# Summing a norm's squares on GpSimd, at later steps, with the inverse norm kept in PSUM

## The chip, the cores and the metric

The program runs on eight cores of one Trainium2 chip, one copy per core, each with its own 2112 tokens; the cores share no data. The metric is the device time of the slowest core in microseconds. Most executions agree within 0.3%, but some fall in a second, slower state, in which one die or both show a lower granted TensorE clock.

Engines are named as in the profile: PE is TensorE, DVE is VectorE, ACT is ScalarE, POOL is GpSimd; SP issues DMAs, PEld is PE's weight load, and a q at the end marks an engine's sequencer. A line in order of time gives start and length in us, engine, line of kernel.py, operation, output<-inputs, shape and count; in brackets stands how long the engine had been idle before and what ended that.

## The reference, cut to what matters

```python
def rmsnorm(x, g):
    xf = x.astype(jnp.float32)
    r = lax.rsqrt(jnp.mean(xf * xf, axis=-1, keepdims=True) + EPS)
    return (xf * r).astype(x.dtype) * g

for l in range(DEPTH):                                   # DEPTH = 4
    h = rmsnorm(x, p['norm1'][l])
    z = h @ p['w_in'][l]
    ...                                                  # pooling, spatial gate, conv: a_out, b_out, c_out
    x = x + jnp.concatenate([a_out, b_out, c_out], axis=-1) @ p['w_out'][l]
    h2 = rmsnorm(x, p['norm2'][l])
    up = h2 @ p['w_up'][l]
    ...                                                  # gated, with a short causal convolution
    x = x + (jax.nn.silu(gate_c) * val) @ p['w_down'][l]
y = rmsnorm(x, p['final_norm'])
```

Model width is 1024, so a column of `x` lies in eight chunks of 128 partitions, and a norm is a sum over partitions and over those eight chunks.

## The kernel before

The tokens are columns: four tiles of 512 and one of 64, which is tile 4, worked in the order 0, 4, 1, 2, 3. Eight norms are woven into the matmul stage that makes their input: four into the output projection (call it O: per step m, 8 matmuls of 512 columns and a DVE add into X) and four into the last group of the down-projection (call it D: 6 matmuls per step). The norm of a tile is one square per chunk on ACT, eight matmuls with a matrix of ones on PE (the sum over partitions, accumulated in a PSUM bank), Ln and Exp on ACT (the inverse norm), and eight applies on DVE.

```python
def bank():                                   # next PSUM bank of 8 in turn, unless reserved
    while True:
        i = pstate["i"] % 8
        pstate["i"] += 1
        if i not in reserved:
            pstate["last"] = i
            return PS[i], RPS[i]

class Norm:
    ...
    def mm(self, ti, kc):                     # one of eight ones-matmuls
        ...                                   # kc == 0: take a bank and reserve it
        S.op("pe", lambda e: e.matmul(pb[:, 0:n], ONES[:], self.sqb[:, q, 0:n], start=(kc == 0), stop=(kc == KC - 1)),
             reads=[self.Rsq[q], Rones], writes=[Rpb])

    def inv(self, ti):
        ...
        S.op("act", lambda e: e.activation(ri, pb[:, 0:n], AF.Ln, bias=EPST[:, 0:1], scale=1.0 / D),
             reads=[Rpb, Rones], writes=[self.Rri[b]])
        reserved.discard(bidx)
        S.op("act", lambda e: e.activation(ri, ri, AF.Exp, scale=-0.5), reads=[self.Rri[b]], writes=[self.Rri[b]])

    def apply(self, ti, kc):                  # H = X * g * ri, one chunk
        ...
        S.op("dve", lambda e: e.scalar_tensor_tensor(dst[:, kc, c0:c0 + n], X[:, kc, c0:c0 + n],
                                                     VT[:, self.gcol + kc:self.gcol + kc + 1], ri, ALU.mult, ALU.mult),
             reads=[RX[kc][ti], self.Rri[b], Rvt], writes=[Rd])

    def step(self, ti, prev, m):              # called in step m of tile ti; prev is the tile before
        self.sq(ti, m)
        if prev is not None:
            if m == 1:
                self.stat(prev)               # the ones-matmuls, then Ln and Exp
            if m >= 2:
                for kc in range((m - 2) * 8 // 6, (m - 1) * 8 // 6):
                    self.apply(prev, kc)
```

`finish(3)`, the norm of the last tile, is called inside the stage that follows. Note that "reserved" is a matter of the order in which the program is written: once the last user of a bank is written down, the bank may be handed out, however far that user lags at run time; a semaphore then makes the new user wait.

## Time and profile before

| | before |
|---|---|
| median of 4 runs, both states | 3044.81 us |
| the two fast runs among them | 2982.6 and 2985.4 us |
| fast runs in the later calls | 2968 to 2977 us |
| stage O, first matmul to the next stage, core 2 | 66.3, 68.4, 69.1, 69.2 us |
| stage D, likewise, first three layers | 56.0, 54.6, 54.9 us |

The stage lengths are read from PE's order of time. They are core 2's, because the cores of the profiled run were not equally clocked; from the view of the cores (span, mean granted clock):

```profile
core 1: 2981.6 us, clock 0.978
core 2: 2957.3 us, clock 0.989
```

Core 1 takes 24 us longer than core 2, with 0.011 less clock.

### The profile page before, as it was taken

The page shows a single profiled execution, that of the slowest core. Times are in us where ns is not written, and L with a number is a line of the kernel's source. Part 1 is how long each engine was busy: PE and PEld are TensorE (multiplying, and loading weights), DVE is VectorE, ACT ScalarE, POOL GpSimd, SP SyncE. Part 2 cuts the span into 40 slices and gives each one's busy share as a digit, 9 for nine tenths or more (in the row PEclk, how much of TensorE's full clock was granted, in tenths as well). Part 3 has the DMA queues.
Part 4 walks back from the last instruction along what each step waited for, and adds up shares of the span by engine and source line. Part 5 has one row for each costly group of instructions (what it writes and reads, how often), then busy time and mean ns, then how long its engine had stood idle before and what let it go on. Part 6 is the DMA issues. An engine that isn't in the chain of part 4 may idle for free.

```text
span 2981.6 us, 48343 instructions; the slowest of 8 cores (2957.3 to 2981.6 us)
## 1 busy us (share of the span) xinstructions
PE 2850.1 (96%) x16064; PEld 1351.3 (45%) x16064; DVE 1711.3 (57%) x3013; ACT 1487.7 (50%) x2645; POOL 201.5 (7%) x408
## 2 busy tenths in 40 slices
PE   2799999999999999999999999999999999999997
PEld 1344444444444444444444544444444544444443
DVE  1634664655664566564665567465567447646466
ACT  2453571736536365371743547264462636627174
POOL 0000010000000010000000001000000000001000
PEclk9888999999999999999999999999999999999999
DMA  6352222222165022222226312222214512222223
GB/s 159 51 109 57 33 42 36 36 36 42 28 114 115 12 48 42 36 36 36 54 34 129 80 25 43 36 36 40 39 34 86 113 39 43 36 36 37 43 44 122
DMA packets 79009, 165.40 MB, mean 55 GB/s; under 512 B 16368, under 2 KB 41328, under 8 KB 78704
## 3 DMA queue, kind: packets, MB, share of 16 engines
q0 software_dynamic: 38208, 108.94, 23.1%
q1 hardware_dynamic: 40560, 53.39, 6.1%
q8 instruction: 135, 2.21, 0.3%
q14 instruction: 106, 0.87, 0.1%
HBM read 246.04 MB, written 27.73 MB: 92 GB/s over the span
## 4 chain that ended last, share of the span: by engine, by line
PE 89%; DVE 4%; DMA 2%; ACT 2%; issue 2%; SPq 1%; DVEq 0%; ACTq 0%
PE ps L835 21%; PE ps L839 21%; PE ps L885 15%; PE ps L792 7%; PE ps L906 6%; PE ps L774 3%; PE ps L671 3%; PE ps L633 2%; PE ps L468 2%; DVE H L379 2%; PE ps L472 2%; PE ps L361 2%; PE ps L760 2%; SPq L138 1%; PE ps L458 1%
## 5 line engine op out<-in xcount | busy, mean ns | idle before, releaser
L835 PE MATMUL ps<-H,wsall 128*128 128x512 bf16 (+1 forms) x3520 | 700.2, 342 | 4.9 <-DVE H L379 4.9
L839 PE MATMUL ps<-H,wsall 128*128 128x512 bf16 (+1 forms) x3520 | 700.2, 342 | 0.0
L849 ACT COPY arena<-ps 128x512 f32<-128x512 f32 (+1 forms) x440 | 224.5, 510 | 623.0 <-PE ps L835 622.6
L854 DVE SCALAR_TENSOR_TENSOR arena<-arena,vt_s 128x512 f32<-128x512 f32 (+1 forms) x440 | 289.2, 657 | 382.4 <-ACT arena L853 381.4
L885 PE MATMUL ps<-arena,wsall 128*128 128x512 bf16 (+1 forms) x2560 | 458.3, 342 | 0.0
L835 PEld LDWEIGHTS ps<-H,wsall 128*128 128x128 bf16 x3520 | 301.2, 98 | 336.3 <-issue 6.8
L839 PEld LDWEIGHTS ps<-H,wsall 128*128 128x128 bf16 x3520 | 302.2, 98 | 332.2
L350 ACT ACTIVATE arena<-X 128x512 bf16<-128x512 f32 (+2 forms) x368 | 194.6, 546 | 341.5 <-DVE X L794 230.1
L853 ACT ACTIVATE arena<-ps,vt_s 128x512 f32<-128x512 f32 (+1 forms) x440 | 310.6, 706 | 65.4 <-ACT arena L849 2.1
L888 DVE TENSOR_TENSOR X<-ps,X 128x512 f32<-128x512 f32 (+1 forms) x320 | 184.7, 596 | 253.2 <-PE ps L885 253.2
L885 PEld LDWEIGHTS ps<-arena,wsall 128*128 128x128 bf16 x2560 | 216.4, 98 | 243.6
L856 DVE SCALAR_TENSOR_TENSOR arena<-arena,vt_s 128x512 f32<-128x512 f32 (+1 forms) x440 | 289.4, 658 | 47.3 <-DVE arena L854 1.8
L379 DVE SCALAR_TENSOR_TENSOR H<-X,vt_s,arena 128x512 bf16<-128x512 f32 (+2 forms) x328 | 211.2, 644 | 132.8 <-ACT arena L372 67.2
L867 DVE TENSOR_TENSOR arena<-arena 128x512 bf16<-128x512 bf16 (+1 forms) x440 | 260.6, 592 | 11.3 <-ACT arena L866 11.0
L866 ACT ACTIVATE arena<-arena 128x512 f32<-128x512 f32 (+1 forms) x440 | 247.2, 562 | 8.6 <-DVE arena L856 8.2
L859 ACT CAST arena<-ps 128x512 bf16<-128x512 f32 (+1 forms) x440 | 224.1, 509 | 54.5 <-PE ps L839 47.7
L792 PE MATMUL ps<-arena,wsall 128*128 128x512 bf16 (+1 forms) x1280 | 242.1, 352 | 0.0
L906 PE MATMUL ps<-arena,wsall 128*128 128x512 bf16 (+1 forms) x960 | 183.2, 352 | 0.0
L792 PEld LDWEIGHTS ps<-arena,wsall 128*128 128x128 bf16 x1280 | 110.5, 100 | 128.6 <-issue 24.3
L794 DVE TENSOR_TENSOR X<-ps,X 128x512 f32<-128x512 f32 (+1 forms) x160 | 94.4, 596 | 101.5 <-PE ps L792 101.4
L361 PE MATMUL ps<-arena,ones 128*128 128x512 bf16 (+2 forms) x368 | 87.3, 353 | 62.5 <-ACT arena L350 56.2
L906 PEld LDWEIGHTS ps<-arena,wsall 128*128 128x128 bf16 x960 | 82.8, 100 | 96.9 <-issue 12.4
(88 smaller groups left out, 2094.8 us busy)
## 6 DMA issues: line engine op xcount, KB each, us to landing
wsall<-wup POOLq DMA_DIRECT2D x88, 512.0 KB, 5.3
wsall<-wdn POOLq DMA_DIRECT2D x32, 512.0 KB, 5.1
arena<-cwd POOLq DMA_DIRECT2D x48, 288.0 KB, 6.5
arena<-hop SPq DMA_DIRECT2D x96, 132.0 KB, 4.0
wsall<-win POOLq DMA_DIRECT2D x16, 512.0 KB, 7.2
y_o<-X SPq DMA_DIRECT2D x8, 1024.0 KB, 4.2
hop<-arena SPq DMA_DIRECT2D x12, 528.0 KB, 6.5
hop<-arena SPq DMA_DIRECT2D x48, 132.0 KB, 2.7
```

Of the source, the lines that this page charges most:

```text
L379: S.op("dve", lambda e: e.scalar_tensor_tensor(dst[:, kc, c0:c0 + n], X[:, kc, c0:c0 + n], VT[:, self.gcol + kc:self.gcol + kc + 1], ri, A ...
L792: S.op("pe", lambda e: e.matmul(pb[:, 0:n], wo[:, kk, ms], rh, start=(q == 0), stop=(q == 7)), reads=[RWS[sl], rr], writes=[Rpb], inc=(q = ...
L835: S.op("pe", lambda e: e.matmul(pg[:, 0:n], wv[:, k, 0:128], H[:, k, c0:c0 + n], start=(k == 0), stop=(k == 7)), reads=[RWS[sl], RH[ti]], ...
L839: S.op("pe", lambda e: e.matmul(pv[:, 0:n], wv[:, k, 128:256], H[:, k, c0:c0 + n], start=(k == 0), stop=(k == 7)), reads=[RWS[sl], RH[ti]] ...
L849: S.op("act", lambda e: e.copy(G[:, gc:gc + n], pg[:, 0:n]), reads=[Rpg], writes=[gw_])
L853: S.op("act", lambda e: e.activation(T_, pg[:, 0:n], AF.Identity, bias=fb, scale=w2), reads=[Rpg, Rvt], writes=[Rtm[q]])
L854: S.op("dve", lambda e: e.scalar_tensor_tensor(T_, G[:, gc - sh:gc - sh + n], w1, T_, ALU.mult, ALU.add), reads=gr_ + [Rvt], writes=[Rtm[q]])
L856: S.op("dve", lambda e: e.scalar_tensor_tensor(T_, G[:, gc - 2 * sh:gc - 2 * sh + n], w0, T_, ALU.mult, ALU.add), reads=gr_ + [Rvt], write ...
L866: S.op("act", lambda e: e.activation(T_, T_, AF.Silu), reads=[Rtm[q]], writes=[Rtm[q]])
L867: S.op("dve", lambda e: e.tensor_tensor(actb[:, fl, c0:c0 + n], VB_, T_, ALU.mult), reads=[Rvst[q], Rtm[q]], writes=[Rab[ti]])
L885: S.op("pe", lambda e: e.matmul(pb[:, 0:n], wd[:, kk, m2 * 128:(m2 + 1) * 128], actb[:, kk, c0:c0 + n], start=(kk == 0), stop=(kk == nf - 1)),
L906: S.op("pe", lambda e: e.matmul(pb[:, 0:n], wvw[:, kk - k0, m * 128:(m + 1) * 128], actb[:, kk, c0:c0 + n], start=(kk == 0), stop=(kk == n ...
```

## The change

It has four parts. **Fold**: GpSimd adds up the squares of seven chunks in fp32 (six adds per 512-column tile, the last one written as bf16), and PE does two ones-matmuls instead of eight. **Times**: the statistics come later, at fixed places, and the applies go one per step through a list. **PSUM**: the inverse norm stays in its PSUM bank, reserved until the last apply is written down. **Weights**: the three loads of feed-forward weights, issued from GpSimd's queue, move from behind stage O into its last tile. The start norm is left unfolded.

```diff
+                if self.fold and kc:
+                    ...
+                    S.op("pool", lambda e: e.tensor_tensor(out, first, sv_, ALU.add), reads=[R0, self.Rsq[q]], writes=[Ro])
             def mm(self, ti, kc):
+                if self.fold:
+                    S.op("pe", lambda e: e.matmul(pb[:, 0:n], ONES[:], self.accb[:, p * 512:p * 512 + n], start=True, stop=False), ...)
+                    S.op("pe", lambda e: e.matmul(pb[:, 0:n], ONES[:], self.s7[:, 0:n], start=False, stop=True), ...)
+                    return
             def inv(self, ti):
-                S.op("act", lambda e: e.activation(ri, pb[:, 0:n], AF.Ln, ...), reads=[Rpb, Rones], writes=[self.Rri[b]])
-                reserved.discard(bidx)
-                S.op("act", lambda e: e.activation(ri, ri, AF.Exp, scale=-0.5), ...)
+                S.op("act", lambda e: e.activation(pb[:, 0:n], pb[:, 0:n], AF.Ln, ...), reads=[Rones], writes=[Rpb])
+                S.op("act", lambda e: e.activation(pb[:, 0:n], pb[:, 0:n], AF.Exp, scale=-0.5), writes=[Rpb])
             def apply(self, ti, kc):
-                ... VT[:, self.gcol + kc:self.gcol + kc + 1], ri, ALU.mult, ALU.mult),
-                     reads=[RX[kc][ti], self.Rri[b], Rvt], writes=[Rd])
+                ... VT[:, self.gcol + kc:self.gcol + kc + 1], pb[:, 0:n], ALU.mult, ALU.mult),
+                     reads=[RX[kc][ti], Rpb, Rvt], writes=[Rd])
+                if kc == KC - 1:
+                    reserved.discard(bidx)
-            def step(self, ti, prev, m):
+            def step(self, ti, m):
                 self.sq(ti, m)
-                ...
+                for t, tp, mp in ((1, 0, 2), (1, 4, 3), (2, 1, 2), (3, 2, 2)):
+                    if (ti, m) == (t, mp):
+                        self.stat(tp)
+                        self.pend += [(tp, kc) for kc in range(KC)]
+                self.drain(self.rate)          # one apply per step; tile 4's count 0.3
     ...
-            for _ in range(3):
-                wload()
+                    if ti == 3 and m in (2, 5, 7):     # inside stage O
+                        wload()
```

More of the change, by code (lines that the diff above doesn't have):

```diff
@@ L336, in build_nc, with __init__ @@
         class Norm:
-            NSQ = 10
-            def __init__(self, gcol, b_sq, b_ri, nsq=NSQ, final=False):
-                self.nsq, self.gcol, self.final = nsq, gcol, final
-                sq_v, self.Rsq = AR.carve("sq", b_sq, nsq * 256, nsq)
-                self.ri, self.Rri = AR.carve("ri", b_ri, 2 * 512, 2)
-                self.sqb = sq_v.bitcast(BF16).rearrange("p (a n) -> p a n", a=nsq)
-                self.i, self.slot, self.bank, self.rb = 0, {}, {}, {}
+            def __init__(self, gcol, base, final=False, fold=True, rate=1.0):
+                self.gcol, self.final, self.fold = gcol, final, fold
+                self.rate, self.credit, self.pend = rate, 0.0, []
+                self.i, self.slot, self.bank, self.par = 0, {}, {}, {}
+                if fold:
+                    self.sqv, self.Rsq = AR.carve("sq", base, 4 * 512, 4)
+                    acc1, Racc1 = AR.carve("acc", base + 2048, 512, 1)
+                    self.acc, self.Racc = [acc1, acc1], [Racc1[0], Racc1[0]]
+                    s4, self.Rs4 = AR.carve("s4", base + 2560, 256, 8)
+                    self.s4 = s4.bitcast(BF16)
+                    s7, self.Rs7 = AR.carve("s7", base + 2816, 256, 1)
+                    self.s7 = s7.bitcast(BF16)
+                    accb, self.Raccb = AR.carve("accb", base + 3072, 2 * 256, 2)
+                    self.accb = accb.bitcast(BF16)
+                else:
+                    sqv, self.Rsq = AR.carve("sq", base, 8 * 256, 8)
+                    self.sqv = sqv.bitcast(BF16)
@@ L346, in sq @@
             def sq(self, ti, kc):
                 c0, n = TTS[ti]
-                q = self.slot[(ti, kc)] = self.i % self.nsq
-                self.i += 1
-                S.op("act", lambda e: e.activation(self.sqb[:, q, 0:n], X[:, kc, c0:c0 + n], AF.Square),
-                     reads=[RX[kc][ti]], writes=[self.Rsq[q]])
+                if self.fold and ti == 4:
+                    S.op("act", lambda e: e.activation(self.s4[:, kc * 64:kc * 64 + 64], X[:, kc, c0:c0 + n], AF.Square),
+                         reads=[RX[kc][ti]], writes=[self.Rs4[kc]])
+                    return
@@ new lines, in sq @@
+                if self.fold and kc == KC - 1:
+                    S.op("act", lambda e: e.activation(self.s7[:, 0:n], X[:, kc, c0:c0 + n], AF.Square),
+                         reads=[RX[kc][ti]], writes=[self.Rs7[0]])
+                    return
+                q = self.slot[(ti, kc)] = self.i % len(self.Rsq)
+                self.i += 1
+                sv_ = self.sqv[:, q * 512:q * 512 + n]
+                S.op("act", lambda e: e.activation(sv_, X[:, kc, c0:c0 + n], AF.Square), reads=[RX[kc][ti]], writes=[self.Rsq[q]])
@@ new lines, in sq @@
+                if self.fold and kc:
+                    p = self.par.setdefault(ti, len(self.par) % 2)
+                    a = self.acc[p][:, 0:n]
+                    first, R0 = a, self.Racc[p]
+                    if kc == 1:
+                        q0 = self.slot[(ti, 0)]
+                        first, R0 = self.sqv[:, q0 * 512:q0 * 512 + n], self.Rsq[q0]
+                    out, Ro = (a, self.Racc[p]) if kc < KC - 2 else (self.accb[:, p * 512:p * 512 + n], self.Raccb[p])
+                    S.op("pool", lambda e: e.tensor_tensor(out, first, sv_, ALU.add), reads=[R0, self.Rsq[q]], writes=[Ro])
@@ L359, in mm @@
                 pb, Rpb, _ = self.bank[ti]
+                if self.fold and ti == 4:
+                    S.op("pe", lambda e: e.matmul(pb[:, 0:n], ONES[:], self.s4[:, kc * 64:kc * 64 + 64], start=(kc == 0), stop=(kc == KC - 1)),
+                         reads=[self.Rs4[kc], Rones], writes=[Rpb])
+                    return
+                if self.fold:
+                    p = self.par[ti]
+                    S.op("pe", lambda e: e.matmul(pb[:, 0:n], ONES[:], self.accb[:, p * 512:p * 512 + n], start=True, stop=False),
+                         reads=[self.Raccb[p], Rones], writes=[Rpb])
+                    S.op("pe", lambda e: e.matmul(pb[:, 0:n], ONES[:], self.s7[:, 0:n], start=False, stop=True),
+                         reads=[self.Rs7[0], Rones], writes=[Rpb])
+                    return
                 q = self.slot[(ti, kc)]
-                S.op("pe", lambda e: e.matmul(pb[:, 0:n], ONES[:], self.sqb[:, q, 0:n], start=(kc == 0), stop=(kc == KC - 1)),
+                S.op("pe", lambda e: e.matmul(pb[:, 0:n], ONES[:], self.sqv[:, q * 512:q * 512 + n], start=(kc == 0), stop=(kc == KC - 1)),
                      reads=[self.Rsq[q], Rones], writes=[Rpb])
@@ L366, in inv @@
                 pb, Rpb, bidx = self.bank[ti]
-                b = self.rb[ti] = len(self.rb) % 2
-                ri = self.ri[:, b * 512:b * 512 + n]
-                S.op("act", lambda e: e.activation(ri, pb[:, 0:n], AF.Ln, bias=EPST[:, 0:1], scale=1.0 / D),
-                     reads=[Rpb, Rones], writes=[self.Rri[b]])
-                reserved.discard(bidx)
-                S.op("act", lambda e: e.activation(ri, ri, AF.Exp, scale=-0.5), reads=[self.Rri[b]], writes=[self.Rri[b]])
+                S.op("act", lambda e: e.activation(pb[:, 0:n], pb[:, 0:n], AF.Ln, bias=EPST[:, 0:1], scale=1.0 / D),
+                     reads=[Rones], writes=[Rpb])
+                S.op("act", lambda e: e.activation(pb[:, 0:n], pb[:, 0:n], AF.Exp, scale=-0.5), writes=[Rpb])
             def apply(self, ti, kc):
                 c0, n = TTS[ti]
-                b = self.rb[ti]
-                ri = self.ri[:, b * 512:b * 512 + n]
+                pb, Rpb, bidx = self.bank[ti]
                 dst, Rd = (X, RX[kc][ti]) if self.final else (H, RH[ti])
                 S.op("dve", lambda e: e.scalar_tensor_tensor(dst[:, kc, c0:c0 + n], X[:, kc, c0:c0 + n],
-                                                             VT[:, self.gcol + kc:self.gcol + kc + 1], ri, ALU.mult, ALU.mult),
-                     reads=[RX[kc][ti], self.Rri[b], Rvt], writes=[Rd])
+                                                             VT[:, self.gcol + kc:self.gcol + kc + 1], pb[:, 0:n], ALU.mult, ALU.mult),
+                     reads=[RX[kc][ti], Rpb, Rvt], writes=[Rd])
+                if kc == KC - 1:
+                    reserved.discard(bidx)
                 if self.final and kc % 4 == 3:
@@ L385, in stat @@
             def stat(self, ti):
-                for kc in range(KC):
+                for kc in range(1 if self.fold and ti != 4 else KC):
                     self.mm(ti, kc)
@@ L391, in finish, with drain @@
                 self.stat(ti)
+                self.drain(100.0)
                 for kc in range(KC):
                     self.apply(ti, kc)
-            def step(self, ti, prev, m):
-                self.sq(ti, m)
-                if prev is not None:
-                    if m == 1:
-                        self.stat(prev)
-                    if m >= 2:
-                        for kc in range((m - 2) * 8 // 6, (m - 1) * 8 // 6):
-                            self.apply(prev, kc)
+            def drain(self, credit):
+                self.credit += credit
+                while self.pend and self.credit > 0:
+                    ti, kc = self.pend.pop(0)
+                    self.apply(ti, kc)
+                    self.credit -= 0.3 if ti == 4 else 1.0
+                self.credit = min(self.credit, 0.0)
+            def step(self, ti, m):
+                self.sq(ti, m)
+                for t, tp, mp in ((1, 0, 2), (1, 4, 3), (2, 1, 2), (3, 2, 2)):
[3 more added lines that the diff above has]
+                self.drain(self.rate)
         def prep_dma(l):
@@ L426, in build_nc @@
         SLB = SGB + 1024
-        nctx = Norm(VT_N1, DGB, AOB, nsq=8)
+        nctx = Norm(VT_N1, DGB, fold=False)
         assert AOB + NT <= AW
@@ L777, in build_nc, with oproj @@
             wload()
-            nctx = Norm(VT_N2 + l * 8, 0, 2560)
+            nctx = Norm(VT_N2 + l * 8, 0)
             wos = [wget(8) for _ in range(3)]
-            def oproj(ti, prev):
+            def oproj(ti):
                 c0, n = TTS[ti]
@@ L795, in oproj @@
                          reads=[Rpb], writes=[RX[m][ti]])
-                    nctx.step(ti, prev, m)
-            for prev, ti in zip([None] + TORD, TORD):
-                oproj(ti, prev)
-            for _ in range(3):
-                wload()
+                    nctx.step(ti, m)
+                    if ti == 3 and m in (2, 5, 7):
+                        wload()
+            for ti in TORD:
+                oproj(ti)
             out_dma(o_conv_o[l], sc_[l][:, 4:30, :], [], "d2d")
@@ L898, in build_nc @@
                     is_fin = (l + 1 == DEPTH)
-                    nctx = Norm(VT_FN if is_fin else VT_N1 + (l + 1) * 8, 0, 2560, final=is_fin)
+                    nctx = Norm(VT_FN if is_fin else VT_N1 + (l + 1) * 8, 0, final=is_fin)
                     for pos, ti in enumerate(TORD):
@@ L910, in build_nc @@
                                  reads=[Rpb], writes=[RX[m][ti]])
-                            nctx.step(ti, TORD[pos - 1] if pos else None, m)
+                            nctx.step(ti, m)
                     if is_fin:
```

## The prediction

> **What bounds the kernel now.** I read the busy table first, then the chain that ended last, the time order of TensorE (PE) through one stage, the windows over it, and last the time order of VectorE (DVE). All rows are core 1, the slowest; fast runs of before took 2982.6 and 2985.4 us, and all times below mean the fast state.
>
> ```profile
> PE 2850.1 (96%) x16064; PEld 1351.3 (45%) x16064; DVE 1711.3 (57%) x3013; ACT 1487.7 (50%) x2645; POOL 201.5 (7%) x408
> ...
> PE 89%; DVE 4%; DMA 2%; ACT 2%; issue 2%; SPq 1%; DVEq 0%; ACTq 0%
> ...
> L361 PE MATMUL ps<-arena,ones 128*128 128x512 bf16 (+2 forms) x368 | 87.3, 353 | 62.5 <-ACT arena L350 56.2
> ```
>
> PE is busy 96% and is 89% of the chain, while POOL has 7%: a PE instruction taken away is time taken away. L361 is the ones-matmul of the norms (sum of squares over partitions): 368 of them, with 62.5 us of waiting in front. Now a down-projection stage of the third layer, in PE's order of time (start, length):
>
> ```profile
> 2208.07 1.89 PE L361 MATMUL ps<-arena,ones 128*128 128x512 bf16 x8
> 2209.80 3.83 PE L906 MATMUL ps<-arena,wsall 128*128 128x64 bf16 x48
> 2213.46 0.25 PE L361 MATMUL ps<-arena,ones 128*128 128x64 bf16 x3
> 2214.23 0.19 PE L361 MATMUL ps<-arena,ones 128*128 128x64 bf16 x1 [0.52 <-ACT arena L350]
> ...
> 2218.64 13.28 PE L906 MATMUL ps<-arena,wsall 128*128 128x512 bf16 x48
> 2231.76 1.89 PE L361 MATMUL ps<-arena,ones 128*128 128x512 bf16 x8
> 2233.49 10.52 PE L906 MATMUL ps<-arena,wsall 128*128 128x512 bf16 x48
> ...
> 2268.10 2.22 PE L458 MATMUL ps<-H,wsall 128*128 128x512 bf16 x6 [2.04 <-DVE H L379]
> ```
>
> Three things: eight ones-matmuls cost 1.73 us of PE (2231.76 to 2233.49), 0.216 each. The eight of the 64-column tile, 0.23 us of work, take from 2213.46 to 2218.64. And the 48 matmuls after them take 13.1 us where the next 48 take 10.4. The windows say why:
>
> ```profile
> 2213.46:2218.64 5.18, 1.16 (x10) 0.65 (x8) 5.08 (x12) 1.29 (x5) 0.00 (x0) 0.88 0.00 2
> 2218.64:2224.00 5.36, 5.36 (x14) 1.87 (x14) 3.02 (x6) 2.32 (x5) 0.00 (x0) 0.50 0.00 0
> ```
>
> In the first stretch PE (first busy figure) has 1.16 of 5.18 us and DVE (third) 5.08; in the second the granted clock, the column after the five engines, is 0.50.
>
> ```profile
> 2213.71 0.75 DVE L379 SCALAR_TENSOR_TENSOR H<-X,vt_s,arena 128x512 bf16<-128x512 f32 x1
> 2214.38 0.22 DVE L909 TENSOR_TENSOR X<-ps,X 128x64 f32<-128x64 f32 x1
> 2214.56 1.61 DVE L379 SCALAR_TENSOR_TENSOR H<-X,vt_s,arena 128x512 bf16<-128x512 f32 x2
> ```
>
> DVE puts the long applies of tile 0 between the short adds of tile 4; tile 4's squares, so its statistic, come at the pace of the applies, and PE stands in its queue.
>
> **What the skill says.** (1) "TensorE: Matmul & The Clock Gate", Part 1: PE's clock falls to half after an idle window of about 3.4 us and needs about as long to come back. The trace agrees: 0.50 for some five us behind that stall. (2) "GPSIMD Engine Reference", 3.1: a two-input fp32 add of 2048 elements took 4497 ns. No row of before shows one; scaled by elements that is 1.12 us for 512, and with semaphores I estimate 1.2 to 1.4. (3) "SBUF — State Buffer", Who interferes with whom: GpSimd blocks against a DVE instruction with two SBUF inputs, not against one with a single SBUF input. The trace fits: the 88 GpSimd copies of 128x32 beside the FFN's two-input DVE work take 209 to 762 ns with a median of 758, for 32 elements, and one DVE instruction there takes 752. The change puts the inverse norm into PSUM, so that every regular DVE instruction of the norm stages has one SBUF input.
>
> **The change, part by part.** There are 8 folded norm stages (4 after the output projection, O; 4 in the last down-projection group, D).
>
> (a) Fold. For each 512-column tile POOL adds up seven squares (6 adds; the eighth goes to PE as it is) and PE does 2 ones-matmuls instead of 8: 6 x 4 x 8 = 192 removed, x 0.216 = 41.5 us, all on PE's path.
>
> (b) Later statistics. Tile 0's statistic moves from the second step of tile 4 to the third of tile 1, so tile 4 meets no applies: DVE needs 8 x about 0.2 us for it, PE 1.4 to 1.9. The stall goes. From the first tile-4 ones-matmul to the next projection matmul, less 0.23: D 4.95, 4.95, 4.95, 4.5; O 2.9, 4.2, 3.8, 3.8: 34 us. The slow clock behind it, against 0.216 per matmul: D 2.3, 1.7, 2.8, 1.7; O 1.7, 1.4, 1.7 (the first layer is held at 0.81 anyway, not counted): 13 us. Together 47.
>
> (c) What it adds. Applies go one per step, so when a stage ends four of tile 2 are still to do (before: none). A step on DVE is one add and one apply, 0.60 + 0.67 = 1.27 us from start to start; PE's step is 8 x 0.216 = 1.73 in O, 6 x 0.216 = 1.30 in D. In O DVE catches up. In D it starts 3 us late (first apply waits for squares, a 1.28 us table load, Ln and Exp), loses another 1 to 1.5 on tile 4's batched applies, and ends about 4 us behind. Then at D's boundary the statistic of tile 3 comes some 1 us late, and four applies x 0.84 us delay H by 3: the wait of 2.04 us at 2268 becomes about 4 in two parts, perhaps with a little more slow clock: 2.5 x 3 = 7.5 us. In O the four fit into the 3.46 us in which PE does the first FFN tile; the present 1.2 us wait stays. A reserved bank given out while its applies lag: 1 us per D, 4. The first FFN weight is issued behind a GpSimd add, 2 to 3 us later than now (now 2 us of slack): 0.5 x 4 = 2. At the end of the program the lag of DVE delays the last applies: 2.
>
> (d) Nothing else: the square takes ACT as long in fp32; applies are bound by 512 elements on DVE with either source; the first norm is unfolded and is set by a 48.6 us wait for a DMA.
>
> Sum: 41.5 + 47 - 7.5 - 4 - 2 - 2 = 73; 2983 - 73 = 2910. I say 2912.
>
> **Rivals.** *POOL becomes the bound.* Six chained adds per tile against 8 steps, 10.8 us in D: the limit is 1.8 us per add, 2.4 in O. My 1.2 to 1.4 leaves room. If adds take 2 us, D alone suffers, by about 1.2 us per tile plus 4 at its end: some 30 us back, 2940. If they block at 3 us, both stages wait for POOL and the time is 2990 or more. Against it: the single SBUF input; for it: spans of POOL are the least sure numbers here, and its queue issues weights too.
>
> *Only the fold counts.* The stall could move instead of go: PE would wait elsewhere for the same DVE work, as applies are postponed, not removed. For it: DVE's step of 1.27 is 98% of PE's in D. Against: in O it is 73%, and of the remainder half runs under the next stage, where evacuation is ACT's. Pure fold: 2983 - 41.5 = 2941; with half of the stalls back, about 2925.
>
> *Clock.* A denser PE could draw a lower granted clock (0.81 is seen in the first layer). One per cent of clock is some 28 us. The 0.98 to 0.99 of all cores argues for little.
>
> **Range and chances.** Both main terms are counted from rows, the costs are estimates with an error of about 15 us, and the first two rivals pull upward. Predicted 2912, range 2882 to 2950. The 2% line is 2924: faster by over 2% 0.68, within 2% 0.30, slower 0.02.
>
> **What would show it.** Ones-matmuls: 368 - 192 = 176. No wait of over 1 us at tile 4's statistic, and clock 1.00 just after. POOL's folds 1.2 to 1.4 us from start to start when back to back, POOL busy 192 x 1.3 = 250 us more. DVE's wait for Exp at tile 1's third step, about 3 us, with no idle PE. At D's boundary a longer wait for H than 2.04. I am wrong if PE waits for GpSimd's sum before its two ones-matmuls in most tiles, if tile 1 to 3 in D run above 11.5 us each, or if the mean granted clock falls.

## The result, and the profile after

The changed kernel is correct. A ratio here is the mean time of one kernel's fast runs over that of the other's fast runs in the same rounds, so it is not quite the ratio of the quoted medians.

| | before | after | ratio, 95% interval |
|---|---|---|---|
| first comparison, median of all runs | 3083.33 us (16 runs) | 2898.51 us (11) | 0.9715 (0.9683 to 0.9747) |
| repeat, on chip 2 | 2970.58 us (7) | 2891.03 us (4) | 0.9731 (0.9707 to 0.9754) |
| second repeat, on chip 7 | 2972.62 us (9) | 2891.30 us (5) | 0.9725 (0.9712 to 0.9739) |
| stage O, core 2 / core 6 | 66.3, 68.4, 69.1, 69.2 | 58.65 each | |
| stage D, core 2 / core 6 | 56.0, 54.6, 54.9 | 46.3, 46.1, 46.1 | |
| feed-forward between O and D, each of four | 431.5 | 430.0 | |
| from D to the next O, each of three | 157.0 to 157.7 | 156.1 to 156.6 | |
| last D with the end of the program | 68.8 | 63.9 | |

In the steadiest call, the last, all nine runs of before were fast: the mean is 2972.6 us against 2890.6 for the four fast runs of after, 82 us. From the page of after: the span, the busy times, the engines of the chain that ended last, and the group of GpSimd's adds:

```profile
span 2884.3 us, 48616 instructions; the slowest of 8 cores (2872.2 to 2884.3 us)
...
PE 2767.3 (96%) x15872; PEld 1321.0 (46%) x15872; DVE 1704.7 (59%) x3013; ACT 1476.3 (51%) x2645; POOL 446.0 (15%) x600
...
PE 88%; DVE 4%; DMA 3%; ACT 2%; SPq 2%; issue 1%; POOL 1%; DVEq 0%; ACTq 0%; POOLq 0%
...
L377 POOL TENSOR_TENSOR arena<-arena 128x512 f32<-128x512 f32 x192 | 244.3, 1272 | 184.1 <-ACT arena L368 167.3
```

PE has exactly 192 instructions fewer and is busy 83 us less; POOL has 192 adds of 1.27 us more; the chain is still PE's. Now the D stage of the third layer again, in PE's order of time (start, length):

```profile
2144.73 0.38 PE L392 MATMUL ps<-arena,ones 128*128 128x512 bf16 x1
...
2146.45 0.40 PE L387 MATMUL ps<-arena,ones 128*128 128x64 bf16 x8
2146.69 9.23 PE L949 MATMUL ps<-arena,wsall 128*128 128x512 bf16 x42
2157.49 0.38 PE L392 MATMUL ps<-arena,ones 128*128 128x512 bf16 x1 [1.58 <-POOL arena L377]
...
2157.93 10.52 PE L949 MATMUL ps<-arena,wsall 128*128 128x512 bf16 x48
...
2188.73 1.46 PE L501 MATMUL ps<-H,wsall 128*128 128x512 bf16 x6 [1.84 <-DVE H L412]
```

Tile 4's eight ones-matmuls, which took from 2213.46 to 2218.64 before, are over in 0.24 us here (2146.45 to 2146.69). The 48 projection matmuls of a tile take 10.4 us. Two waits are left: 1.58 us for GpSimd's sum at the second statistic, and 1.84 us for H in the next stage, against 2.04 before. The windows over the first statistic (busy time of PE, PEld, DVE, ACT, POOL, then the granted clock):

```profile
2144.73:2149.90 5.17, 5.17 (x32) 2.49 (x31) 1.32 (x2) 3.65 (x5) 2.54 (x2) 1.00 0.00 0
2149.90:2157.49 7.59, 6.01 (x28) 2.57 (x27) 7.59 (x14) 3.98 (x8) 5.09 (x4) 1.00 0.00 0
```

DVE still stands in the first stretch (1.32 busy of 5.17 us, it waits for Exp), but PE is full and the clock stays 1.00. In the second stretch DVE is busy all the time.

At the boundary of that stage, DVE's order of time, before first and then after:

```profile
2260.76 1.60 DVE L379 SCALAR_TENSOR_TENSOR H<-X,vt_s,arena 128x512 bf16<-128x512 f32 x2 [4.04 <-ACT arena L372]
```

```profile
2177.68 3.30 DVE L412 SCALAR_TENSOR_TENSOR H<-X,vt_s,ps 128x512 bf16<-128x512 f32 x4
2181.52 1.60 DVE L412 SCALAR_TENSOR_TENSOR H<-X,vt_s,ps 128x512 bf16<-128x512 f32 x2 [0.54 <-ACT ps L406]
```

Before, DVE stood 4.04 us for the last tile's Exp. After, it does its four left-over applies in that time (3.30 us) and still waits 0.54: the left-over work fills a hole and delays nothing.

At the end of the program the last statistic of the run, in the order of time of PE, POOL and DVE of after, then DVE's of before:

```profile
2870.73 0.58 PE L392 MATMUL ps<-arena,ones 128*128 128x512 bf16 x1 [4.03 <-DVE X L412]
```

```profile
2869.21 1.27 POOL L377 TENSOR_TENSOR arena<-arena 128x512 bf16<-128x512 f32 x1 [0.27 <-ACT arena L362]
```

```profile
2873.28 6.70 DVE L412 SCALAR_TENSOR_TENSOR X<-X,vt_s,ps 128x512 f32<-128x512 f32 x8 [0.96 <-ACT ps L406]
```

```profile
2971.77 5.39 DVE L379 SCALAR_TENSOR_TENSOR X<-X,vt_s,arena 128x512 f32<-128x512 f32 x8 [1.54 <-ACT arena L372]
```

PE stands 4.03 us. The profile names a DVE apply, but GpSimd's last add ends at 2870.48, 0.25 us before PE starts: that is the later of the two. Then the last eight applies take 6.70 us instead of 5.39: each waits for the one before, because the program's record of a PSUM bank lets one reader in at a time. (A run below, in which they wait once for Exp, shows them 0.66 us apart.)

### The profile page after: what moved, and what is told of

It reads as the page before. It is cut to its first block, busy times and chain, and to the rows that moved or that the text cites. A ratio compares the mean times of both kernels' runs of the same rounds, so it can differ in the third digit from the quotient of the medians.

```text
span 2884.3 us, 48616 instructions; the slowest of 8 cores (2872.2 to 2884.3 us)
## 1 busy us (share of the span) xinstructions
PE 2767.3 (96%) x15872; PEld 1321.0 (46%) x15872; DVE 1704.7 (59%) x3013; ACT 1476.3 (51%) x2645; POOL 446.0 (15%) x600
## 4 chain that ended last, share of the span: by engine, by line
PE 88%; DVE 4%; DMA 3%; ACT 2%; SPq 2%; issue 1%; POOL 1%; DVEq 0%; ACTq 0%; POOLq 0%
PE ps L878 21%; PE ps L882 21%; PE ps L928 16%; PE ps L835 8%; PE ps L949 4%; PE ps L817 3%; PE ps L714 3%; DVE H L412 2%; PE ps L511 2%; PE ps L515 2%; PE ps L676 2%; PE ps L803 2%; SPq L138 2%; DMA hop<-arena 1%; DMA arena<-cwd 1%
## 5 line engine op out<-in xcount | busy, mean ns | idle before, releaser
L928 PE MATMUL ps<-arena,wsall 128*128 128x512 bf16 (+1 forms) x2560 | 458.3, 342 | 0.0
L928 PEld LDWEIGHTS ps<-arena,wsall 128*128 128x128 bf16 x2560 | 216.4, 98 | 243.6
L899 DVE SCALAR_TENSOR_TENSOR arena<-arena,vt_s 128x512 f32<-128x512 f32 (+1 forms) x440 | 289.4, 658 | 47.3 <-DVE arena L897 1.8
L368 ACT ACTIVATE arena<-X 128x512 f32<-128x512 f32 (+3 forms) x272 | 159.9, 604 | 250.9 <-DVE X L837 169.5
L412 DVE SCALAR_TENSOR_TENSOR H<-X,vt_s,ps 128x512 bf16<-128x512 f32 (+2 forms) x328 | 208.6, 638 | 114.3 <-DMA cvq_s<-cvq 49.3
L377 POOL TENSOR_TENSOR arena<-arena 128x512 f32<-128x512 f32 x192 | 244.3, 1272 | 184.1 <-ACT arena L368 167.3
L835 PE MATMUL ps<-arena,wsall 128*128 128x512 bf16 (+1 forms) x1280 | 231.7, 342 | 0.0
L949 PE MATMUL ps<-arena,wsall 128*128 128x512 bf16 (+1 forms) x960 | 174.6, 342 | 0.0
L835 PEld LDWEIGHTS ps<-arena,wsall 128*128 128x128 bf16 x1280 | 107.4, 98 | 119.9
L837 DVE TENSOR_TENSOR X<-ps,X 128x512 f32<-128x512 f32 (+1 forms) x160 | 93.8, 595 | 68.1 <-PE ps L835 67.4
L904 POOL COPY arena<-arena 128x2 f32<-128x2 f32 x88 | 20.1, 229 | 700.9 <-ACT arena L892 700.9
```

Of the source, the lines that this page charges most:

```text
L377: S.op("pool", lambda e: e.tensor_tensor(out, first, sv_, ALU.add), reads=[R0, self.Rsq[q]], writes=[Ro])
L835: S.op("pe", lambda e: e.matmul(pb[:, 0:n], wo[:, kk, ms], rh, start=(q == 0), stop=(q == 7)), reads=[RWS[sl], rr], writes=[Rpb], inc=(q = ...
L899: S.op("dve", lambda e: e.scalar_tensor_tensor(T_, G[:, gc - 2 * sh:gc - 2 * sh + n], w0, T_, ALU.mult, ALU.add), reads=gr_ + [Rvt], write ...
L928: S.op("pe", lambda e: e.matmul(pb[:, 0:n], wd[:, kk, m2 * 128:(m2 + 1) * 128], actb[:, kk, c0:c0 + n], start=(kk == 0), stop=(kk == nf - 1)),
L949: S.op("pe", lambda e: e.matmul(pb[:, 0:n], wvw[:, kk - k0, m * 128:(m + 1) * 128], actb[:, kk, c0:c0 + n], start=(kk == 0), stop=(kk == n ...
```

## The experiments

Fold (F), times (T) and PSUM (P) can be switched one by one, so the first question is whether their gains add, as the prediction let them. In all these kernels the weights are issued as in after, so every ratio to before contains that part too; no run moves the weights alone.

**The changed kernel again**, beside the first experiments.

> The changed kernel once more, as the neighbour on the same chip for the next three. Expected 0.9715 of before within its interval, 2880 to 2910 us in the fast state; PE waits 1.6 us for GpSimd in each D stage and 4 us at the very end, none at tile 4.

Measured: 2891.03 us, ratio 0.9731 (0.9707 to 0.9754).

**Fold and PSUM at the old times (F + P).**

```diff
-                for t, tp, mp in ((1, 0, 2), (1, 4, 3), (2, 1, 2), (3, 2, 2)): ...
-                self.drain(self.rate)
+                prev = {0: None, 4: 0, 1: 4, 2: 1, 3: 2}[ti]
+                if prev is not None:
+                    if m == 1:
+                        self.stat(prev)
+                    if m >= 2:
+                        for kc in range((m - 2) * 8 // 6, (m - 1) * 8 // 6):
+                            self.apply(prev, kc)
```

> Fold kept, statistics and applies at the old places. My theory (two separate gains: 41.5 us of removed matmuls, 47 us of removed stalls and slow clock): only the first is left, and tile 0's statistic, now due one step into tile 4, also waits for the last adds on GpSimd: about 40 to 55 us slower than the changed kernel, ratio to before 0.985 to 0.992; clock 0.50 again behind tile 4. Rival (only the fold counts, the new places move the stall elsewhere): within 5 us of the changed kernel.

Measured: 3015.26 us, ratio 1.0154 (1.0136 to 1.0172). A miss: slower than before, where a gain was expected. PE's order of time at the start of tile 4 in a D stage:

```profile
778.00 0.58 PE L392 MATMUL ps<-arena,ones 128*128 128x512 bf16 x1 [4.31 <-POOL arena L377]
...
788.78 2.72 PE L951 MATMUL ps<-arena,wsall 128*128 128x512 bf16 x6 [5.29 <-DVE H L412]
```

Two waits stand where one stall stood before. At the old time the sum is not ready: GpSimd's six adds stand back to back, some 1.47 us from start to start (1.27 and a gap of 0.20), and the last ends at 777.75, 0.25 us before PE starts. And a projection matmul waits 5.29 us for an apply. A projection matmul reads no H here, so it waits for a bank: which part does that is for the next runs.

**PSUM alone (P)**, twice.

```diff
-                if self.fold and kc:          # no adds on GpSimd; eight ones-matmuls; old times as above
+                if False:
```

> Before with one part of the change alone: inverse norm in PSUM, so its bank is held until the tile's last apply; no fold, old places. The run of the fold at old places was 46 us slower than before, with 62 us of PE waits at projection matmuls for DVE applies (a held bank handed out again while its applies lag). If those waits come from the bank, they show here too: 15 to 40 us slower than before, ratio 1.005 to 1.013, PE idle at projection matmuls for DVE applies. If they came from the fold's lateness: within 5 us of before.

> The inverse norm in PSUM alone, at the old times and unfolded, which had only one fast run. If that run was right: ratio to before 1.015 to 1.020. If it was not: 1.005 to 1.013, as first expected.

Measured: first a lowest time of 3025.3 us, then 3026.65 us, ratio 1.0184 (1.0170 to 1.0198). The sign was expected, the size was not: 54 us lost. PE and DVE, in order of time, repeat run:

```profile
780.76 2.51 PE L956 MATMUL ps<-arena,wsall 128*128 128x64 bf16 x42
790.69 2.72 PE L956 MATMUL ps<-arena,wsall 128*128 128x512 bf16 x6 [7.42 <-DVE H L417]
```

```profile
788.84 1.60 DVE L417 SCALAR_TENSOR_TENSOR H<-X,vt_s,ps 128x512 bf16<-128x512 f32 x2
```

Tile 4's 42 matmuls take PE 2.51 us, and in that time the order of the program uses up the bank of tile 0: its last apply has been written down, so it is handed out. But DVE's last apply of it ends only at 790.44, and PE starts 0.25 us later, after 7.42 us of waiting. That settles the second wait of F + P: it is the price of the bank. Over the program PE waits 67.4 us for applies at projection matmuls here (29.0 in O, 38.4 in D), and none of the listed waits of before is of this kind.

**New times and PSUM without the fold (T + P)**, and **new times alone (T)** with the inverse norm in SBUF.

```diff
-                if self.fold and kc:
+                if False:                      # T + P
-                S.op("act", lambda e: e.activation(pb[:, 0:n], pb[:, 0:n], AF.Exp, scale=-0.5), writes=[Rpb])
+                S.op("act", lambda e: e.activation(ri, ri, AF.Exp, scale=-0.5), ...)   # T: also this
```

> New places of statistics and applies, but no fold: eight ones-matmuls per tile again, GpSimd idle. My theory: about 41 us slower than the changed kernel less some 6 us of waits for GpSimd and 3 at the end that it does not have, so 30 to 40 us; ratio to before 0.982 to 0.986; no stall at tile 4 and clock 1.00 there. Rival (only the fold counts): as before, ratio 0.995 to 1.005.

> New places alone: inverse norm in SBUF as before, no fold. Without GpSimd work nobody competes for SBUF, so the PSUM part should not matter: as the run with new places and PSUM but no fold, ratio 0.982 to 0.986 to before (stall and slow clock behind tile 4 gone, 47 us). If the PSUM inverse is itself a gain: 0.988 to 1.0.

Measured: T + P 2925.94 us, ratio 0.9842 (0.9823 to 0.9862); T 0.9854 (0.9832 to 0.9876), its three fast runs 2926.7 to 2932.0. Both hit. With the new times the bank costs nothing (0.9842 and 0.9854 overlap), since applies go one per step of a 512-column tile and don't lag. And the fold, added to T + P, gives 0.9842 less 0.9731, 33 us.

**Fold alone (F)**, old times, inverse norm in SBUF.

```diff
     ...                                          # old times and ri in SBUF, as in before
+                if self.fold and kc: ... S.op("pool", ... ALU.add)      # against before: only the fold is added
```

> Fold alone: old places, inverse norm in SBUF (bank freed after Ln). No bank waits, but tile 0's statistic waits some 4 us for GpSimd one step into tile 4, the stall at tile 4 stays, and applies with two SBUF inputs are stretched beside the adds to about 1.15 us: 41.5 us of matmuls removed, some 4 x 8 of waits and 20 to 40 of stretched applies added, ratio 0.99 to 1.01. Rival (the fold's gain is independent of the other two parts): 0.986.

Measured: 2992.29 us, ratio 1.0066 (1.0043 to 1.0089), within what was expected: the fold by itself gains nothing. Its groups of ones-matmuls (busy, mean ns, idle time before them):

```profile
L395 PE MATMUL ps<-arena,ones 128*128 128x512 bf16 x32 | 13.2, 412 | 55.8 <-POOL arena L380 47.3 <-DVE H L426 8.4
...
L390 PE MATMUL ps<-arena,ones 128*128 128x64 bf16 x64 | 7.9, 192 | 22.6 <-ACT arena L361 22.6
```

The 41 us of PE work are gone, but PE stands 47.3 us for GpSimd's sums, and the stall at tile 4 (22.6 us) is still there. Its applies with both inputs in SBUF also take 930 ns on average beside the adds, where before has 749.

**Fold and new times, inverse norm in SBUF (F + T).**

```diff
+                    S.op("act", lambda e: e.activation(ri, pb[:, 0:n], AF.Ln, ...), reads=[Rpb, Rones], writes=[self.Rri[b]])
+                    reserved.discard(bidx)
+                    S.op("act", lambda e: e.activation(ri, ri, AF.Exp, scale=-0.5), ...)
+                    return
```

> Changed kernel with the inverse norm in SBUF again (two buffers as before), so each apply has two SBUF inputs while GpSimd adds. Theory of the shared read interface: the adds go from 1.48 us apart to 1.8 to 2.2 where applies run, applies get longer too, PE waits for GpSimd in D grow from 1.6 to 3 to 8 us: 10 to 40 us slower than the changed kernel. Rival (PSUM only frees SBUF space): within 4 us of it.

Measured: 2945.06 us, ratio 0.9911 (0.9891 to 0.9930). That is 54 us over the changed kernel, above the expected 10 to 40. The applies, the adds and PE's wait before the ones-matmuls, by shape, here, and then the applies in after (the start norm keeps its inverse in PSUM, so x224 stands against x248):

```profile
L426 DVE SCALAR_TENSOR_TENSOR H<-X,vt_s,arena 128x512 bf16<-128x512 f32 x224 | 213.0, 952 | 40.4 <-ACT arena L413 32.4 <-DVE H L426 0.5 <-DVE arena L883 0.4
...
L380 POOL TENSOR_TENSOR arena<-arena 128x512 f32<-128x512 f32 x160 | 211.5, 1322 | 202.3 <-ACT arena L371 193.3 <-POOL arena L380 8.4 <-ACT arena L361 0.6
...
L395 PE MATMUL ps<-arena,ones 128*128 128x512 bf16 x32 | 12.7, 397 | 30.2 <-POOL arena L380 21.2 <-ACT arena L365 9.1
```

```profile
L412 DVE SCALAR_TENSOR_TENSOR H<-X,vt_s,ps 128x512 bf16<-128x512 f32 x248 | 183.9, 741 | 59.2 <-ACT ps L406 49.0 <-DVE H L412 0.5 <-DVE arena L869 0.4
```

With both inputs in SBUF an apply takes 952 ns on average instead of 741, while the add goes from 1272 only to 1322. DVE is the loser of the two. In D, an add into X and an apply then cost DVE up to 1.68 us against PE's 1.30, the squares come late, and PE waits 30.2 us before the ones-matmuls (10.6 in after). Waits for the first FFN weight (8.1 us) and some 8 us more for H come on top; the rest of the 54 us is not traced. The Trainium skill, "SBUF — State Buffer", section "Who interferes with whom", has the rule that such a DVE instruction contends with GpSimd's reads and one with a single SBUF input does not. The trace agrees with both halves: with the inverse norm in PSUM the 741 ns are no more than the 749 of before, where GpSimd adds nothing up.

So, in ratios to before: P 1.018, F 1.007, F + P 1.015, T 0.985, T + P 0.984, F + T 0.991, and all three 0.973. The gains don't add. The fold needs the new times to have GpSimd's sum ready, and PSUM to keep DVE clear of GpSimd; PSUM needs the new times to have its bank free.

**Weights behind the stage**, as in before.

```diff
-                    if ti == 3 and m in (2, 5, 7):
-                        wload()
+            for _ in range(3):
+                wload()
```

> Changed kernel with the three FFN weight loads issued after the O stage as before, so behind all of GpSimd's adds. If that part of the change matters: the first load starts some 2 us after the stage's last matmul, lands 5 to 6 us later, PE stands about 7 us at the first FFN matmul of each of 4 layers and comes back at half clock: 25 to 40 us slower than the changed kernel. If the adds are done in time for the load: within 4 us.

Measured: 2932.40 us, ratio 0.9864 (0.9848 to 0.9881), some 40 us over the changed kernel, at the upper end of what was expected. PE and POOL in order of time at an O boundary:

```profile
1032.08 3.57 PE L878 MATMUL ps<-H,wsall 128*128 128x512 bf16 x8 [8.19 <-DMA wsall<-wup]
```

```profile
1025.15 1.64 POOL L138 DMA_DIRECT2D wsall<-wup  x3
```

GpSimd issues these loads only when its last add is done, at 1025.15, and PE waits 8.19 us for the first: 33.1 us over the four layers. The small diff about the weights is what keeps the fold from losing its gain.

**Every add done twice**, to see what slower adds would do.

```diff
+                    S.op("pool", lambda e: e.tensor_tensor(self.dum, first, sv_, ALU.add), ...)
                     S.op("pool", lambda e: e.tensor_tensor(out, first, sv_, ALU.add), ...)
```

> Every add on GpSimd issued twice (the first into a tile nobody reads), so about 2.96 us per folded square. My limit from the prediction was 1.8 us per add in D and 2.4 in O: both are exceeded, GpSimd needs 4 x 6 x 2.96 = 71 us for a stage of 46 (D) or 59 (O): 80 to 130 us slower than the changed kernel, waits of PE for GpSimd in both stages. If GpSimd has hidden slack: under 30 us, in D alone.

Measured: 3034.38 us, ratio 1.0210 (1.0195 to 1.0225), 143 us over the changed kernel, more than the expected 80 to 130. The first of each pair of ones-matmuls (busy, mean ns, idle time before them):

```profile
L394 PE MATMUL ps<-arena,ones 128*128 128x512 bf16 x32 | 15.4, 481 | 119.2 <-POOL arena L379 116.8 <-DVE H L414 2.5
```

PE waits 116.8 us for the sums. Twelve adds of 1.27 us take GpSimd at least 15.2 us per tile, where PE's eight steps take 10.4 us in D and 13.8 in O, so GpSimd becomes the bound. The real fold's six adds, 1.48 us apart, need 8.9 us of the 10.4 in D.

**Half a fold**: three adds on GpSimd and five ones-matmuls.

```diff
-                if self.fold and kc == KC - 1:
+                if self.fold and kc >= 4:      # chunks 4 to 7 go to PE as they are
```

> GpSimd adds only the first four squares of a tile (3 adds), the other four go to PE as they are: 5 ones-matmuls per tile instead of 2. 3 x 0.216 x 32 = 20.7 us more of PE, less the waits for GpSimd that vanish (1.6 x 4 in D, 4 at the end): 10 to 17 us slower than the changed kernel. If the gain of the fold is not proportional to the matmuls removed: within 4 us.

Measured: two fast runs near 2902 and 2908 us, ratio of fast runs 0.9776 (0.9756 to 0.9797). About 13 us over the changed kernel, as expected: half of the removed matmuls, less a part of the waits.

**An earlier first statistic in D, and a lighter end of the program**, both together; then **the lighter end alone**, beside both others on one chip.

```diff
-                if self.fold and kc == KC - 1:
+                if self.fold and kc == KC - 1 and not (self.final and ti == 3):   # the end: last tile unfolded
+                Rinv = self.Rinv[ti] = Res("inv")
+                Rinv.w = Rpb.w
-                     reads=[RX[kc][ti], Rpb, Rvt], writes=[Rd])
+                     reads=[RX[kc][ti], self.Rinv[ti] if kc < KC - 1 else Rpb, Rvt], writes=[Rd])  # wait once for Exp
-                for t, tp, mp in ((1, 0, 2), ...
+                for t, tp, mp in ((1, 0, 1), ... if self.early else ((1, 0, 2), ...               # D only
-                self.drain(self.rate)
+                if not (self.early and ti == 1 and m in (1, 2)):
+                    self.drain(self.rate)
```

> Three repairs to the changed kernel: in D the statistic of tile 0 one step earlier and its first apply one step later, so DVE does not stand for Exp; in the very last tile no fold; applies wait once for Exp and not for each other through the bank. Expected: the 1.6 us wait for GpSimd in each D and the 4 us at the end gone, 6 to 11 us faster than the changed kernel. If the late waits are not set by the lag of DVE: within 3 us.

> The changed kernel itself, as the base of this call. Ratio to before 0.970 to 0.974.

> Only the end of the program is mended: the last tile of the last norm unfolded (eight ones-matmuls, no GpSimd sum), and its applies wait once for Exp instead of one for the other. In this trace PE waited 4.03 us for GpSimd's last add there and the last eight applies took 6.70 us instead of 5.39. Theory that the end of the program is most of what earlier statistics and this mending gained together: 4 to 6 us under the changed kernel, ratio to it 0.998 to 0.9986, and less than 3 us left between this and the kernel with both edits. Rival, that the in-stage wait of 1.58 us at the second statistic of the down-projection (four times) is as much: 2 us here and another 5 with both edits.

> Both edits, repeated beside the changed kernel: 6 to 10 us under it, ratio to it 0.9965 to 0.998.

Measured: both edits 2883.25 us, ratio 0.9704 (0.9684 to 0.9723). In the last call the changed kernel has 0.9725 (0.9712 to 0.9739), the end alone 2887.14 us and 0.9709 (0.9696 to 0.9723), both edits 2882.97 us and 0.9697 (0.9684 to 0.9710). In means of fast runs that is 2890.6, 2885.8 and 2882.6: 4.8 us for the end of the program, another 3.2 for the first statistic. These differences of means are about as large as the spread of single runs (some 5 us), so the stages of the three profiles are the better measure, as means over the eight cores: the last D with the end of the program takes 63.7, 60.9 and 59.9 us, the other D stages 46.2, 46.2 and 45.2. By them the end is worth 2.8 us and the first statistic 4.0 (1.0 in each of the four D stages). The second is more than the "less than 3" that the first theory gave it and less than its rival's 5. The gain of both edits over the changed kernel is 8.0 us here; by ratios (0.9704 and 0.9731) it is 8. PE's ones-matmuls on GpSimd's sum, end alone, then both:

```profile
L403 PE MATMUL ps<-arena,ones 128*128 128x512 bf16 x31 | 11.7, 378 | 6.6 <-POOL arena L384 6.3
```

```profile
L403 PE MATMUL ps<-arena,ones 128*128 128x512 bf16 x31 | 11.7, 379 | 2.2 <-POOL arena L384 2.1
```

The 6.3 us are the four waits of D; with the earlier statistic 2.1 us are left, at the first statistic. DVE at the end of the program, end alone:

```profile
2869.69 8.64 DVE L425 SCALAR_TENSOR_TENSOR X<-X,vt_s,ps 128x512 f32<-128x512 f32 x13
```

The 13 applies now stand 0.66 us apart, as those of before did (5.39 us for eight). The version with both edits beats the changed kernel and the kernel before.

**One step further**: the last tile's statistic also earlier in the next stage.

```diff
-                        if f == 0 and ti == 0:          # feed-forward: after the value half
-                            nctx.finish(3)
+                        if f == 0 and ti == 0:          # between gate half and value half
+                            nctx.finish(3)
-                    if pos == 1:                        # behind D: the same, one tile earlier
+                    if pos == 0:
```

> The version with early statistic and unfolded last tile, and besides the last tile's statistic placed earlier in the next stage: after the gate half of the first FFN tile instead of after both halves, and after the first input-projection block instead of the second. H of the last tile is then ready 1.7 us earlier in O, 0.5 in D; the waits of 1.0 us (4 times) and 1.5 us (3 times) shrink: 3 to 6 us faster than that version, ratio to before 0.967 to 0.970. If something else sets those waits: no change.

Measured: 2894.66 us, ratio 0.9739 (0.9720 to 0.9758), a miss: slower than without it. The value half's matmuls have 11.1 us of waits on applies over the four layers; the first of them:

```profile
324.48 2.48 PE L898 MATMUL ps<-H,wsall 128*128 128x512 bf16 x8 [2.73 <-DVE H L425]
```

PE waits 2.73 us for an apply and then takes 2.48 us for matmuls that take 1.89 elsewhere. That it is again a bank in use, as with PSUM alone, fits the order of the program; no run here shows it apart.

## Why the prediction was right or wrong

Two steps failed. The first is the base, which was never turned into a ratio. The second is term (c) of the sum, "What it adds": it charged 15.5 us, where the stages show about 9.5, and none of its four entries came about as described. Term (b) held, and (a) held with the other parts present, though not alone.

**The base.** The prediction took 2983 us, "the fast state", as its start and handed in 2912. Fast against fast that is a ratio of 0.976, where 0.9715 was measured, and 2898.5 lies in its range. But set against the 3044.81 given as the time before, a median of both states, 2912 claims 4.4%, which no fast comparison shows: they show 2.7 to 2.9%, and 0.9715 of 3044.81 is 2958, above the range. The gain itself was also larger than the sum: 82 us, against 73.

**(a) Fold, 41.5 us, and (b) later statistics, 47 us: right.** PE lost 192 instructions, and the tile-4 stall and the half clock behind it are gone. By stages, core 2 against core 6: of the fold's 32 statistics, 21 lie inside the first four O and three D stages (27 us), and (b) put 41 us there; less 3 us for the bank that makes 65 us, and 65.5 were gained (O 38.5, D 27.0). So close a match is partly luck: (b) was read on core 1, the gain on core 2, and against core 1's own stages of before it is 68.8. Seven more statistics, those of the last tiles, lie in the stage that follows: 9.1 us forecast, 9.2 gained (6.0 in the feed-forward stages, 3.1 in the others). What was missing is not the size but a condition. T alone gave 1.46%, 43 us, so (b) holds by itself; the fold gave 33 us on top of T + P, and nothing alone: "all on PE's path" is true of the matmuls, but at the old times PE waits there for GpSimd's sums instead (47.3 us).

**(c) What it adds, 15.5 us: mis-sized, term by term.**
- "2.5 x 3 = 7.5 us" at D's boundary: nothing. The wait for H was 1.48 to 1.84 us, not above the 2.04 of before. The step "four applies x 0.84 us delay H by 3" added DVE's lag to a wait for Exp that was there anyway; the applies ran inside it.
- "A reserved bank given out while its applies lag: 1 us per D": no such wait with the new times. In its place PE waits 1.58 us per D for GpSimd's sum at the second statistic. DVE stands 3.6 us for the first Exp with its adds into X queued behind, so the squares and the folds start late; an earlier statistic cut these waits from 6.3 to 2.1 us in all.
- "The first FFN weight ... 0.5 x 4 = 2": no wait on that DMA in after. The prediction saw a small cost where the edit saves 40 us, since it did not ask what the old place would cost behind GpSimd's adds.
- "At the end of the program ... 2": the last D with the end was forecast to gain 5.2 + 6.2 - 1 - 2 = 8.4 us and gained 4.9, so the term is 5.5. PE stood for GpSimd's last add there (4.03 us), which the prediction did not have; mending the end gave 2.8 us back by the stages, 4.8 by means of fast runs.

The boundary and the weights were charged 9.5 us too much, the end 3.5 too little: 73 + 6 = 79 us, and the stages from the first O on sum to 65.5 + 9.2 + 4.9 = 79.6. The means of fast runs give 82; the 2 to 3 us between are not explained, and single cores differ by more (the first O begins between 247 and 268 us over the cores of the two profiles, without order).

**(d) "Nothing else": held.** No stage outside these moved by more than its statistic and 0.2 us. Of the signs it named, the adds came slower than "1.2 to 1.4 us from start to start", at 1.48, and the wait for H at D's boundary did not grow; the others came true.

**The rivals.** "Only the fold counts ... Pure fold: 2941" was wrong in the way that taught most: the fold alone is slower than before. "POOL becomes the bound" did not come. Its upper case was borne out: with every add done twice the time is 3034, where the rival said 2990 or more for 3 us per add; its limits of 1.8 and 2.4 us lie between the two and were not tested. "Clock" went the other way: over all cores of the fast runs of the last call the mean granted clock was 0.9872 before and 0.9925 after.

## What to carry to other kernels

Work moved to an idle engine pays only if its result is ready when the busy engine asks for it, if the buffers it needs are free, and if it does not disturb the engine beside it: switch such parts one by one, since here two of three lose time alone. Before charging a lag to a later wait, look at what that wait is for; work that fits inside it costs nothing. And say which state of the chip a predicted time belongs to, and give the ratio with it.

## What the Trainium skill lacked or had wrong

- "SBUF — State Buffer", "Who interferes with whom": says that a DVE instruction with two SBUF inputs contends with GpSimd's reads, but lacks a size for a stream of them: beside chained GpSimd adds, DVE's applies went from 741 to 952 ns on average and the adds only from 1272 to 1322 ns, so DVE paid most of it (47 us over 224 applies, 8 us over 160 adds).
- "GPSIMD Engine Reference", 3.1: gives 4497 ns for an fp32 add of 2048 elements, which scales to 1.12 us for 512. Measured: 1.27 us, and 0.20 us more before the next add that depends on it, 1.48 from start to start. The section names GpSimd's dispatch of each instruction but has no figure for it, so scaling by elements falls 0.15 us short.
- "TensorE: Matmul & The Clock Gate", Part 1: gives an idle window of about 3.4 us and mentions that frequent short idles can also lower the clock, but not how busy PE may be in such a window. In the kernel before the clock fell to 0.50 after a stretch of 5.18 us in which PE was busy 1.16 us in single short matmuls and no idle gap was longer than 1.52 us.
- No page has that a PSUM bank kept for a result becomes, when the rotation of eight comes round to it, a wait for its last reader: 7.42 us at one place and 54 us over the program with PSUM alone. "PSUM — Partial Sum Buffer", in its summary, only advises to evacuate promptly.
